# Both projections with 512-column matmuls, low parts of plain weight blocks by ScalarE and an accumulating DMA, bias rows copied DRAM to DRAM

## The chip, the cores and the metric

The kernel runs on one core of a Trainium2 chip. The metric is the device time of one execution in microseconds (us), the median of several runs. Engines: TensorE (PE in the profile), VectorE (DVE), ScalarE (ACT), GpSimd (POOL, used here almost only to issue DMAs) and SyncE (SP, which issues the loads of weights). Each engine works through its own instructions in order and waits on semaphores for the others.

## What is computed

One decoder layer on 512 tokens of width 2048, all in float32: an input projection (2048 to 12288), a gated convolution and three dilated attentions with a relative-position bias, an output projection (2048 to 2048), a LayerNorm, an up projection (2048 to 11264), a gated convolution with SiLU, a down projection (5632 to 2048) and a second LayerNorm.

```
proj = x @ w_in                                   # 512 x 2048 @ 2048 x 12288
u, gate_b, gate_c, q, k, v = split(proj)
y_conv = gate_b * causal_conv3(gate_c * u, conv_mix_w)
y_attn = mix of three dilated window attentions (scores + bias(rel_bias))
x1 = layernorm(ALPHA * x + concat(y_conv, y_attn) @ w_out)
up = causal_conv3(x1 @ w_up, ffn_conv_w) + ffn_conv_b     # 2048 x 11264
a, g = split(up)
out = layernorm(ALPHA * x1 + (silu(g) * a) @ w_down)
```

The change touches the two widest products, `x @ w_in` and `x1 @ w_up` ("both projections"), and the table of bias rows.

## The kernel before

**Two-part numbers.** A float32 operand is cut into a high part, rounded to fp32r by ScalarE, and a low part, the rest. A product is three matmuls: high by high, high weight by low activation, low weight by high activation.

**Both projections** take the output features in pairs of two 128-feature blocks: 48 pairs for `w_in` (phase 1), 44 for `w_up` (phase 3; each pair is a value block and its gate block). Tokens are cut into two halves of 256, the 2048 inputs into two halves of 1024, so that a pair is a 2 x 2 by 2 x 2 block product. It is computed with seven products instead of eight (Winograd's form of Strassen's method). `PROD` lists them: product 1 is A11 by B11, 5 is S1 by T1, 6 is S2 by T2, 3 is S4 by B22, 7 is S3 by T3, 4 is A22 by T4, 2 is A12 by B21. The activations' S are sums of token blocks, computed once per phase; the weights' T are differences of weight blocks, computed anew for every pair by VectorE. The order is `MAIN` = 1, 5, 6, 3, 7, 4, 2, below called steps 0 to 6. Steps 0, 3 and 6 use a plain weight block (kind "B"), the other four a T.

**One product** (`product`, lines 317 to 329) is 8 chunks of three matmuls of 256 columns, weights stationary: `op.hi` by the activation's high part (326), `op.hi` by its low part (327), `op.lo` by its high part (328). All three add into one half of a PSUM bank; a pair uses two banks, "m" for the sums x2 and x1, "n" for x4 and x3. ScalarE copies some of the running sums out in between (`snap`, 374), and VectorE adds copy and bank to the output tile o (`bands`, 572 and 581).

**Weight preparation** (`Op`, lines 162 to 196). `front` computes T where there is one (VectorE, 181) and the high part (ScalarE, 191); `back` computes the low part (VectorE, 194). High and low tiles lie in a ring of `RING` = 4, so the front of a weight block is issued when PE has finished the product four steps earlier, and its back when the next front has been issued. Raw weights are loaded by SP into `RAWS` = 3 tiles of 1 MB; a tile is loaded anew when every part made of it is done.

**After a pair** `later(n, ...)` and `tick` put work some products later into the program. In phase 3 `done3` issues, one step after the next pair's step 0, two scaled copies by ScalarE (1006); the convolution's taps by VectorE (589), SiLU by ScalarE (1010), the gate's product by VectorE (1013) and a store to `act_d` by POOL (1014) follow in the next three steps. In phase 1 `done1` stores q, k, v to `qkv_d` by POOL (611) or runs the mixer's convolution.

**A few pairs are different.** At the start of each phase five pairs have products 1 and 2 taken ahead (`run_pre`) and one pair is computed with the plain eight products (`run_plain`), while S and T operands aren't there yet. That leaves 42 of 48 pairs in phase 1 and 38 of 44 in phase 3 with all seven products in `run_pairs`.

**Bias rows** (`bias_setup`, 548): in phase 1, after the last mixer pair, three small tables of 8 heads by up to 383 values are computed in an o tile on 8 partitions, and POOL writes each to `seq_d` in DRAM with every row repeated 128 times (563). The attention reads them later with a skewed access pattern.

The output and down projections (`tm_unit`, lines 421 to 423) use 512-column matmuls with the activations stationary; their weights have kind "W".

Of the kernel before, what the change touches and what calls it, by code (L numbers as in the profile page):

```python
# [12 lines left out]
F32 = mybir.dt.float32  # L13
# [5 lines left out]
P = 128  # L19
D = 2048  # L20
S = 512
# [32 lines left out]
UNIT = 1024  # L54
NWARM = 6
XS, XL, XF, XR = 4, (0, 0, 1, 4), (1, 2, 3, 6), (7, 9, 11, 12)
HF, HR = 3, (6, 8, 10, 12)
# [17 lines left out]
def _plain(seq):  # L75
    return isinstance(seq[0], str)
# [5 lines left out]


class Chunks:
    def __init__(self, tiles, j):
        self.tiles, self.j = tiles, j

    def __getitem__(self, at):
        k = at[1]
        if isinstance(k, slice):  # L90
            return self.tiles[k.start // 2][:, self.j]
        return self.tiles[k // 2][:, self.j, k % 2]


@with_exitstack
def layer_kernel(ctx: ExitStack, tc: tile.TileContext, xT, x, w_in, w_out, w_up, w_down, cw, fw, lnp, lnc, table,
# [32 lines left out]
    act_d = dram.tile([P, FT, S], F32, name="act_d")  # L129
    seq_d = dram.tile([3, NH, P, 384], F32, name="seq_d")  # L130
    stA_d = dram.tile([NH, S, 2], F32, name="stA_d")
    stB_d = dram.tile([NH, S, 2], F32, name="stB_d")
# [29 lines left out]
    class Op:  # L162
        def __init__(self, kind, parts, box=None, ext=0):
            self.kind, self.parts, self.box, self.ext = kind, parts, box, ext
            for r, _ in parts:
                r.left += 1
            ops.append(self)
# [8 lines left out]
        def front(self):  # L176
            v = [self.view(i) for i in range(len(self.parts))]
            if self.kind[0] == "T":
                self.src = tt_tile()
                prev = v[1] if len(v) > 1 else self.box["T1" if self.kind == "T2" else "T2"]  # L180
                nc.vector.tensor_sub(self.src, v[0], prev)  # L181
# [9 lines left out]
            nc.scalar.activation(self.hi, self.src, AF.Copy)  # L191

        def back(self):
            nc.vector.tensor_sub(self.lo, self.src, self.hi.bitcast(F32))  # L194
            for r, _ in self.parts:
                r.left -= 1
# [110 lines left out]
    pairb = {}  # L307

    def region(p, name):
        rg = pairb.setdefault(p, {})  # L310
# [6 lines left out]
    def product(p, q, X, last):  # L317
        op = take()
        for q in q if isinstance(q, str) else [q]:
            xn, _, reg = PROD[q]  # L320
            xh, xl = X[xn]
            first = not _banks(q) & set(pairb.get(p, {}))
# [42 lines left out]

    def run_pairs(pl, X, stile, otile, bands, done, hook=None):
        for p, seq, pre in pl:
            if pre or _plain(seq):
                continue
            sn = {b: stile(b).rearrange("p (a t) -> p a t", a=2) for b in "mn"}  # L370
# [69 lines left out]
    def s_alloc(X, pools):  # L440
        for n in ("S2", "S4"):
            tiles = [None] * 4
            X[n] = (Chunks(tiles, 0), Chunks(tiles, 1))
        X["pools"] = pools
# [29 lines left out]
    def xtile(pool, n):  # L474
        return tuple(pool.tile([P, 8, 256], F32R, tag=n + s, name=nm(n + s)) for s in "hl")

# [54 lines left out]
    hook = schedule(todo)  # L531

    def keep1():
        return tp.tile([P, 2, 256], F32, tag="kp", name=nm("kp"), bufs=PRE1[0])

# [4 lines left out]
    nc.sync.dma_start(gb_t, lnc)  # L540

    def stile1(b):
        return tp.tile([P, 512], F32, tag="s" + b, name=nm("s" + b), bufs=2)

# [3 lines left out]
    def bias_setup(g=0):  # L548
# [9 lines left out]
        def finish():  # L558
# [16 lines left out]
    def bands1(p, o, b, ps, sn):  # L575
# [3 lines left out]
        for i in range(2):  # L579
            f, h = (i, i) if b == "m" else (i, 1 - i)  # L580
            nc.vector.tensor_add(ov[:, f, :, 64 * h:64 * h + 64],
                                 ps[:, 256 * i:256 * i + 256].rearrange("p (m r) -> p r m", r=4),
                                 sn[:, i].rearrange("p (m r) -> p r m", r=4))

    held = {}
# [26 lines left out]

    run_plain(plan1, X, otile1, done1, hook)
    run_pairs(plan1, X, stile1, otile1, bands1, done1)
    ph1.close()

# [217 lines left out]
    a1p = mkpool(a1s, "a1p")  # L834
    A1h = a1p.tile([P, 2, 8, 256], F32R, tag="h", name="A1h")
    A1l = a1p.tile([P, 2, 8, 256], F32R, tag="l", name="A1l")
    chp = mkpool(chs, "chp")
# [125 lines left out]
    X["S3"] = xtile(s3p, "S3")  # L963
    X["A11"], X["A12"] = (A1h[:, 0], A1l[:, 0]), (A1h[:, 1], A1l[:, 1])

# [23 lines left out]
    def act_first(p, q):  # L989
        if p < FT - 1:  # L990
            return
        if q == 2:
            act_load(0, xrp, "S1h", nc.gpsimd)
            act_load(1, xrp, "S1l", nc.gpsimd)
            for s in "hl":
                act[s] = a1p.tile([P, 2, 4, S], F32R, tag=s, name=nm("A" + s))
        if q in (6, 3):
# [22 lines left out]
    run_plain(plan3, X, otile3, done3, hook)  # L1020
    run_pairs(plan3, X, stile3, otile3, bands, done3, act_first)
    xrs.close()
# [177 lines left out]
```

## Time and profile before

| what | time |
|---|---|
| median of 3 runs | 2673.99 us (2672.46 to 2676.10) |
| the profiled execution, whole | 2674.91 us |
| its span | 2673.0 us, mean granted TensorE clock 0.992 |
| phase 1 (`w_in`) | from the start to about 1020 us |
| attention and output projection | about 1020 to 1290 us |
| phase 3 (`w_up`) | about 1260 to 2110 us |
| down projection, second LayerNorm | about 2110 to 2673 us |

The page lists the busy time of each engine, then the span in 40 slices, the DMA queues, the chain of waits that ended last, groups of instructions by line, and DMA issues. In a row of a group, "out<-in" are tile names, then come partitions x elements, the count, busy us and mean ns. Consecutive instructions of one engine overlap a little, so the mean of one is slightly more than the step from one to the next. A row of the stretches lists, for a window of the span, the busy us and the number of instructions of each engine, the granted clock, the DMA engines' share and GB/s.

### The profile page before, as it was taken

What the parts mean: (1) busy time and instruction counts of PE and PEld (TensorE: products, weight loads), DVE (VectorE), ACT (ScalarE), POOL (GpSimd) and SP (SyncE); (2) the same over time, 40 slices, a digit from 0 to 9 for tenths busy, and PEclk for the clock granted to TensorE, in tenths of its full rate; (3) what the DMA queues carried; (4) which work ended last, traced back from release to release, by engine and by line L of the source; (5) the groups of instructions that cost most, each with busy time, mean ns of one, the idle gap of its engine ahead of it and who ended that gap; (6) DMA issues with size and microseconds to landing.
All of it is one profiled execution on the core that took longest, in us unless ns stands there. A gap on an engine that the chain in (4) does not pass through costs nothing.

```text
span 2673.0 us, 45078 instructions
## 1 busy us (share of the span) xinstructions
PE 2624.3 (98%) x19114; PEld 2497.2 (93%) x19114; DVE 2015.5 (75%) x2293; ACT 1159.3 (43%) x1617; POOL 124.4 (5%) x214
## 2 busy tenths in 40 slices
PE   9999889999999999999999999999999999999998
PEld 8999789999999998888999999999999998888886
DVE  7987557777777777666899888888888875675557
ACT  5444334444444444434655555555555553222220
POOL 0000000000000002221000000000000000000000
PEclk9999989999999999999999999999999999999999
DMA  7433653333333338644543333333333354434331
GB/s 240 166 103 128 111 138 125 134 129 132 135 123 139 134 119 312 221 160 160 182 144 131 117 123 111 123 123 108 126 119 111 127 181 156 149 142 148 120 126 63
DMA packets 70905, 376.69 MB, mean 141 GB/s; under 512 B 10608, under 2 KB 14440, under 8 KB 36016
## 3 DMA queue, kind: packets, MB, share of 16 engines
q1 hardware_dynamic: 51680, 311.47, 34.0%
q0 software_dynamic: 19024, 62.34, 7.3%
q8 instruction: 150, 2.46, 0.4%
q14 instruction: 51, 0.42, 0.1%
HBM read 324.95 MB, written 48.81 MB: 140 GB/s over the span
## 4 chain that ended last, share of the span: by engine, by line
PE 88%; DVE 5%; DMA 4%; ACT 1%; issue 1%; SPq 0%; DVEq 0%; POOL 0%; ACTq 0%
PE bk L326 21%; PE bk L328 21%; PE bk L327 21%; PE bk L423 8%; PE bk L421 8%; PE bk L422 8%; DMA raw<-in_w_in_dram 2%; DMA seq_d<-o 2%; DVE wlo L194 1%; DVE tt L181 1%; PE bk L744 1%; PE bk L690 1%; PE bk L674 0%; ACT whi L191 0%; PE bk L736 0%
## 5 line engine op out<-in xcount | busy, mean ns | idle before, releaser
L191 ACT ACTIVATE whi<-raw 128x1024 fp32r<-128x1024 f32 x394 | 416.0, 1058 | 631.9 <-PE bk L423 219.0
L194 DVE TENSOR_TENSOR wlo<-raw,whi 128x1024 fp32r<-128x1024 f32 x394 | 480.7, 1223 | 216.0 <-ACT whi L191 215.9
L194 DVE TENSOR_TENSOR wlo<-tt,whi 128x1024 fp32r<-128x1024 f32 x360 | 440.5, 1224 | 210.1 <-ACT whi L191 209.5
L191 ACT ACTIVATE whi<-tt 128x1024 fp32r<-128x1024 f32 x360 | 379.6, 1054 | 220.1 <-PE bk L327 122.7
L326 PE MATMUL bk<-S,whi 128*128 128x256 f32 x1440 | 409.2, 284 | 12.4 <-ACT sm L374 11.5
L327 PE MATMUL bk<-S,whi 128*128 128x256 f32 x1440 | 408.4, 284 | 0.0
L328 PE MATMUL bk<-S,wlo 128*128 128x256 f32 x1440 | 408.4, 284 | 0.0
L326 PEld LDWEIGHTS bk<-S,whi 128*128 128x128 f32 x1440 | 277.5, 193 | 13.6 <-ACT sm L374 11.9
L327 PEld LDWEIGHTS bk<-S,whi 128*128 128x128 f32 x1440 | 277.5, 193 | 0.0
L328 PEld LDWEIGHTS bk<-S,wlo 128*128 128x128 f32 x1440 | 277.4, 193 | 0.0
L181 DVE TENSOR_TENSOR tt<-raw,tt 128x1024 f32<-128x1024 f32 x180 | 219.1, 1217 | 36.6 <-DMA raw<-in_w_in_dram 36.6
L326 PE MATMUL bk<-A22h,whi 128*128 128x256 f32 x752 | 212.8, 283 | 0.0
L327 PE MATMUL bk<-A22l,whi 128*128 128x256 f32 x752 | 212.8, 283 | 0.0
L328 PE MATMUL bk<-S3h,wlo 128*128 128x256 f32 x752 | 212.8, 283 | 0.0
L327 PE MATMUL bk<-S3l,whi 128*128 128x256 f32 x752 | 212.8, 283 | 0.0
L326 PE MATMUL bk<-S3h,whi 128*128 128x256 f32 x752 | 212.8, 283 | 0.0
L328 PE MATMUL bk<-A22h,wlo 128*128 128x256 f32 x752 | 212.8, 283 | 0.0
L328 PE MATMUL bk<-S1h,wlo 128*128 128x256 f32 x720 | 205.1, 285 | 6.2 <-DVE wlo L194 6.2
L326 PE MATMUL bk<-A1h,whi 128*128 128x256 f32 x720 | 205.2, 285 | 0.6 <-ACT S L932 0.6
L326 PE MATMUL bk<-S1h,whi 128*128 128x256 f32 x720 | 204.7, 284 | 0.0
L327 PE MATMUL bk<-S1l,whi 128*128 128x256 f32 x720 | 204.7, 284 | 0.0
L328 PE MATMUL bk<-A1h,wlo 128*128 128x256 f32 x720 | 204.4, 284 | 0.0
(225 smaller groups left out, 6435.4 us busy)
## 6 DMA issues: line engine op xcount, KB each, us to landing
raw<-in_w_in_dram SPq DMA_DIRECT2D x97, 1024.0 KB, 4.9
raw<-in_w_up_dram SPq DMA_DIRECT2D x89, 1024.0 KB, 5.3
raw<-in_w_down_dram SPq DMA_DIRECT2D x44, 1024.0 KB, 4.9
qkv_d<-o POOLq DMA_DIRECT2D x36, 512.0 KB, 4.3
raw<-in_w_out_dram SPq DMA_DIRECT2D x16, 1024.0 KB, 6.8
act_d<-z POOLq DMA_DIRECT2D x44, 256.0 KB, 5.2
qk<-qkv_d SPq DMA_DIRECT2D x7, 1536.0 KB, 10.3
ar<-act_d SPq DMA_DIRECT2D x9, 1024.0 KB, 7.0
```

Of the source, the lines that this page charges most:

```text
L181: nc.vector.tensor_sub(self.src, v[0], prev)
L191: nc.scalar.activation(self.hi, self.src, AF.Copy)
L194: nc.vector.tensor_sub(self.lo, self.src, self.hi.bitcast(F32))
L326: mm(ps, op.hi[:, w], xh[:, k], start=first and k == 0, stop=False, skip_group_check=True)
L327: mm(ps, op.hi[:, w], xl[:, k], start=False, stop=False, skip_group_check=True)
L328: mm(ps, op.lo[:, w], xh[:, k], start=False, stop=last and k == 7, skip_group_check=True)
L421: mm(banks[n], yh[:, tt], op.hi[:, w], start=first and i == 0, stop=False)
L422: mm(banks[n], yh[:, tt], op.lo[:, w], start=False, stop=False)
L423: mm(banks[n], yl[:, tt], op.hi[:, w], start=False, stop=last and i == 1)
L690: mm(ps[:, o:o + P], qk[:, 2 + 2 * g, rs], qk[:, 3 + 2 * g, rs], start=True, stop=True)
L744: nc.tensor.transpose(ps[:, i * P:(i + 1) * P], src[:, n, s:s + P], ident)
```

## The change

It has four parts.

1. **Wide products.** For pairs that have all seven products, `run_wide` and `product_wide` replace `run_pairs`' loop and `product`. High and low part of an activation now lie in one tile (`Wide`, `WideChunks`; method `both`), and one matmul of 512 columns multiplies `op.hi` with both. It writes a whole bank: the left half holds high by high, the right half high by low. The third matmul, `op.lo` by the high part, still has 256 columns and adds into the right half. A product is 8 x (512 + 256) columns in 16 matmuls instead of 24 of 256. A pair uses four banks, x1 to x4.
2. **Combining.** ScalarE copies whole banks (512 columns) after steps 0, 1 and 2, and x1 once more into a tile "u" in step 6. Each of the four 256-token blocks of a pair is then an addition of 512 columns (bank plus copy) and an addition of the two halves into o, both on VectorE. The block (f, h) = (0, 1), which uses u, is combined in step 6 and (0, 0) in the next pair's step 0. Tiles of the copies have their own tags in phase 1 and share the z tiles in phase 3.
3. **Low parts of plain blocks.** For weight blocks of kind "B", from the ninth on (`NLOW` = 8), `front` lets ScalarE write the negated rounded value into the low tile, and `back` issues, from POOL, a DMA of 512 KB from SBUF to SBUF that adds the raw weights to it. T blocks and the kind "W" keep VectorE's subtraction.
4. **Bias rows.** The small table goes to `seq1_d` first (8 rows), and a second DMA, DRAM to DRAM, writes the 128 copies to `seq_d` with the copies' index outermost.

Three places of the order of instructions, before and after. The first is ScalarE in phase 3, from the last instruction of step 6 of one pair on (before), and from the weight block issued in step 6 on (after). whi and wlo are high and low tiles, bk a PSUM bank, z a copy of a bank or a scaled copy of o. Before:

```order
L191 ACTIVATE whi_17823<-raw_17670 128x1024
L374 ACTIVATE z_17829<-bk_2193_17831 128x256
L191 ACTIVATE whi_17859<-tt_17857 128x1024
L1006 ACTIVATE z_17864<-o_17827,fw_t 128x512
L1006 ACTIVATE z_17865<-o_17827,fw_t 128x512
L374 ACTIVATE z_17829<-bk_2199_17868 128x256
L191 ACTIVATE whi_17896<-tt_17894 128x1024
L1010 ACTIVATE z_17865<-z_17865 128x512
L374 ACTIVATE z_17830<-bk_2193_17831 128x256
L191 ACTIVATE whi_17930<-raw_17670 128x1024
```

After, the same stretch:

```order
L220 ACTIVATE whi_14689<-raw_14567 128x1024
L222 ACTIVATE wlo_14690<-raw_14567 128x1024
L432 ACTIVATE z_14694<-bk_2248_14511 128x512
L454 ACTIVATE z_14715<-bk_2279_14698 128x512
L220 ACTIVATE whi_14719<-tt_14717 128x1024
L1120 ACTIVATE z_14725<-o_14644,fw_t 128x512
L1120 ACTIVATE z_14726<-o_14644,fw_t 128x512
L454 ACTIVATE z_14746<-bk_2286_14729 128x512
L220 ACTIVATE whi_14750<-tt_14748 128x1024
L1124 ACTIVATE z_14726<-z_14726 128x512
L454 ACTIVATE z_14775<-bk_2279_14698 128x512
L220 ACTIVATE whi_14777<-raw_14567 128x1024
```

New are the negated copy (L222) and, behind it, the copy u of x1 (L432); the copies of banks are twice as wide.

The second place is VectorE in phase 3 around the same point: tt are the T blocks. Before, from the first `bands` of a pair to the taps of its two blocks:

```order
L572 TENSOR_TENSOR o_19207<-bk_2334_19018,z_18980 128x512
L181 TENSOR_TENSOR tt_19237<-raw_18884,raw_19050 128x1024
L194 TENSOR_TENSOR wlo_19204<-raw_19050,whi_19203 128x1024
L572 TENSOR_TENSOR o_19207<-bk_2328_18981,z_18979 128x2x256
L181 TENSOR_TENSOR tt_19274<-raw_19050,tt_19173 128x1024
L194 TENSOR_TENSOR wlo_19240<-tt_19237,whi_19239 128x1024
L589 SCALAR_TENSOR_TENSOR z_19245<-o_19207,fw_t,z_19245 128x511
L589 SCALAR_TENSOR_TENSOR z_19245<-o_19207,fw_t,z_19245 128x510
L194 TENSOR_TENSOR wlo_19277<-tt_19274,whi_19276 128x1024
```

After, from the second block of a pair to the taps of its gate (z_15629 is u):

```order
L435 TENSOR_TENSOR z_15494<-bk_2403_15446,z_15494 128x512
L1137 TENSOR_TENSOR o_15579<-z_15494 128x256
L228 TENSOR_TENSOR wlo_15602<-tt_15599,whi_15601 128x1024
L435 TENSOR_TENSOR z_15629<-bk_2426_15582,z_15629 128x512
L1137 TENSOR_TENSOR o_15579<-z_15629 128x256
L210 TENSOR_TENSOR tt_15652<-raw_15366,raw_15502 128x1024
L435 TENSOR_TENSOR z_15463<-bk_2430_15607,z_15463 128x512
L1137 TENSOR_TENSOR o_15579<-z_15463 128x256
L210 TENSOR_TENSOR tt_15683<-raw_15502,tt_15599 128x1024
L228 TENSOR_TENSOR wlo_15655<-tt_15652,whi_15654 128x1024
L701 SCALAR_TENSOR_TENSOR z_15661<-o_15579,fw_t,z_15661 128x511
L701 SCALAR_TENSOR_TENSOR z_15661<-o_15579,fw_t,z_15661 128x510
```

The low part of a plain block is gone from VectorE; the addition that reads u stands ahead of T3 (L210, tt_15652) and of the last block's additions.

The third place is POOL at the bias rows. Before:

```order
L606 DMA yc_d<-o_2942 128x1024
L551 DMA tb<-in_table_dram 32x24
L563 DMA seq_d<-o_2983 1024x1x383
L611 DMA qkv_d<-o_3172 128x2x512
L563 DMA seq_d<-o_3208 1024x1x255
```

After:

```order
L226 DMA wlo_2776<-raw_2568 128x1024
L226 DMA wlo_2797<-raw_2618 128x1024
L664 DMA seq_d<-o_2727 8x383
L665 DMA seq_d<-seq_d 128x8x383
L226 DMA wlo_2876<-raw_2755 128x1024
L723 DMA qkv_d<-o_2825 128x2x512
L226 DMA wlo_2961<-raw_2755 128x1024
```

The first L664 row writes `seq1_d`. The accumulating DMAs (L226) share POOL's queue with both copies of the bias rows and with the stores.

The core of the diff:

```diff
+NLOW = 8
+    def product_wide(p, q, X, last):
+        op = take()
+        xn, _, reg = PROD[q]
+        first = reg not in pairb.get(p, {})
+        ps = wide_region(p, reg)
+        for k in range(8):
+            w = slice(k * P, (k + 1) * P)
+            mm(ps.rearrange("p (a t) -> p a t", a=2), op.hi[:, w], X[xn].both(k), start=first and k == 0, stop=False,
+               skip_group_check=True)
+            mm(ps[:, 256:], op.lo[:, w], X[xn][0][:, k], start=False, stop=last and k == 7, skip_group_check=True)
+        return op
...
+    WSUM = {(0, 0): ("x2", 1), (1, 1): ("x1", 5), (0, 1): ("x4", "x1"), (1, 0): ("x3", 6)}
+    def run_wide(p, seq, X, stile, otile, put_block, done, hook):
+        WNEED = {(0, 0): {1, 2}, (1, 1): {5, 6, 7}, (0, 1): {4, 6, 7}, (1, 0): {3, 6}}
+        def combine(block):
...
+            reg, other = WSUM[block]
+            if other == "x1":
+                u = stile("u")
+                nc.scalar.activation(u, pairb[p][other], AF.Copy)
+            else:
+                u = sn[other]
+            nc.vector.tensor_add(u, pairb[p][reg], u)
+            put_block(p, box["o"], block, u)
...
+            op = product_wide(p, q, X, PROD[q][2] not in {PROD[j][2] for j in left})
+            if q in (1, 5, 6):
+                sn[q] = stile(str(q))
+                nc.scalar.activation(sn[q], pairb[p][PROD[q][2]], AF.Copy)
+            for block, need in WNEED.items():
+                if block not in sent and not need & left:
+                    sent.add(block)
+                    later(2, functools.partial(combine, block))
+            free(op)
+            tick()
...
+            self.by_dma = kind[0] == "B" and len(ops) >= NLOW
...
             nc.scalar.activation(self.hi, self.src, AF.Copy)
+            if self.by_dma:
+                nc.scalar.activation(self.lo, self.src, AF.Copy, scale=-1.0)
 
         def back(self):
-            nc.vector.tensor_sub(self.lo, self.src, self.hi.bitcast(F32))
+            if self.by_dma:
+                nc.gpsimd.dma_start(self.lo, self.src, accum_op=OP.add)
+            else:
+                nc.vector.tensor_sub(self.lo, self.src, self.hi.bitcast(F32))
...
-            nc.gpsimd.dma_start(seq_d[g, :, :, :b - a], mk[:, None].to_broadcast([NH, P, b - a]))
+            nc.gpsimd.dma_start(seq1_d[g, :, :b - a], mk)
+            nc.gpsimd.dma_start(seq_d[g, :, :, :b - a].rearrange("h p n -> p h n"),
+                                seq1_d[g, None, :, :b - a].to_broadcast([P, NH, b - a]))
...
+    def block3(p, o, block, u):
+        f, h = block
+        nc.vector.tensor_add(o[:, 2 * f + h], u[:, :256], u[:, 256:])
```

`block1`, its counterpart in phase 1, writes with a stride of four tokens for the dilated groups. The remaining lines put the two parts of each activation operand into one tile.

More of the change, by code (lines that the diff above doesn't have):

```diff
@@ L80, in _banks, with __init__, __getitem__, both @@
     return {"m" if PROD[i][2] in ("x1", "x2") else "n" for i in (q if isinstance(q, str) else [q])}
+class Wide:
+    def __init__(self, t):
+        self.t = t
+    def __getitem__(self, j):
+        return self.t[:, j]
+    def both(self, k):
+        return self.t[:, :, k]
 class Chunks:
@@ L92, in __getitem__, with __init__, both @@
         return self.tiles[k // 2][:, self.j, k % 2]
+class WideChunks:
+    def __init__(self, tiles):
+        self.tiles = tiles
+    def __getitem__(self, j):
+        return Chunks(self.tiles, j)
+    def both(self, k):
+        return self.tiles[k // 2][:, :, k % 2]
 @with_exitstack
@@ L474, in xtile @@
     def xtile(pool, n):
-        return tuple(pool.tile([P, 8, 256], F32R, tag=n + s, name=nm(n + s)) for s in "hl")
+        return Wide(pool.tile([P, 2, 8, 256], F32R, tag=n, name=nm(n)))
     ph1 = ExitStack()
@@ L992, in act_first @@
         if q == 2:
[L993 to L996, printed above, removed]
+            t = xrp.tile([P, 2, 4, S], F32, tag="S1", name=nm("ar"))
+            for i in range(2):
+                act[i] = t[:, i]
+                nc.gpsimd.dma_start(act[i], act_d[:, 4 * i:4 * i + 4, :])
+            t = a1p.tile([P, 2, 2, 4, S], F32R, tag="A1", name=nm("A"))
+            act["h"], act["l"] = t[:, 0], t[:, 1]
         if q in (6, 3):
@@ L1020, in layer_kernel @@
     run_plain(plan3, X, otile3, done3, hook)
-    run_pairs(plan3, X, stile3, otile3, bands, done3, act_first)
+    def block3(p, o, block, u):
+        f, h = block
+        nc.vector.tensor_add(o[:, 2 * f + h], u[:, :256], u[:, 256:])
+    run_pairs(plan3, X, stile3, otile3, bands, done3, act_first, block3)
     xrs.close()
```

54 lines of the change are left out of this document (44 added, 10 removed).

## The prediction

> **What bounds the kernel now.** First the page's engines and its chain of waits.
>
> ```profile
> PE 2624.3 (98%) x19114; PEld 2497.2 (93%) x19114; DVE 2015.5 (75%) x2293; ACT 1159.3 (43%) x1617; POOL 124.4 (5%) x214
> PE 88%; DVE 5%; DMA 4%; ACT 1%; issue 1%; SPq 0%; DVEq 0%; POOL 0%; ACTq 0%
> ```
>
> PE is busy nearly always, and the chain of waits runs through PE for 88%. But a busy PE is no measure of its pace, so next come stretches of the span: us, then busy us (and count) of PE, PEld, DVE, ACT, POOL, the granted clock, the DMA share, GB/s.
>
> ```profile
> 0.00:70.00 70.00, 63.56 (x470) 60.68 (x471) 54.86 (x68) 39.44 (x54) 0.70 (x6) 0.98 0.68 231
> 270.00:400.00 130.00, 106.30 (x808) 103.30 (x808) 71.45 (x71) 39.77 (x52) 6.96 (x8) 0.89 0.58 125
> 400.00:700.00 300.00, 300.00 (x2502) 300.00 (x2502) 220.29 (x214) 126.28 (x163) 10.00 (x14) 1.00 0.37 130
> 1400.00:2080.00 680.00, 679.75 (x5664) 679.54 (x5664) 597.45 (x614) 356.75 (x474) 18.92 (x35) 1.00 0.36 120
> 2200.00:2600.00 400.00, 400.00 (x1766) 331.22 (x1765) 234.06 (x275) 104.09 (x107) 6.45 (x12) 1.00 0.39 142
> ```
>
> In phase 1, 2502 matmuls of 256 columns in 300 us are one per 119.9 ns; phase 3 has 5664 in 680 us, 120.1 ns. The down projection's 512-column matmuls come every 226.5 ns. Twice the columns cost 106.6 ns more, so 13.3 ns of each matmul don't depend on its columns. PE sets the pace in both phases; VectorE is at 73% and 88%, ScalarE at 42% and 52%. From 270 to 400 us PE does 808 matmuls where 130 us hold 1084: 276 x 0.1199 = 33 us are lost there, the only large hole. Those losing it, from the list of waits (waiter, released by: total us, times, longest):
>
> ```profile
> DVE tt L181 <- DMA raw<-in_w_in_dram: 36.6, 3, 15.5
> DVE o L572 <- DMA seq_d<-o: 11.7, 1, 11.7
> PE bk L326 <- ACT sm L374: 11.5, 2, 10.6
> ```
>
> While the bias rows are written, raw weights come late and o stays occupied.
>
> **Wide matmuls.** A product's chunk was three matmuls, 359.7 ns; now it is 226.5 + 119.9 = 346.4. A step takes 8 x 346.4 ns = 2.77 us for 2.88, a pair of seven steps 19.40 for 20.14: 0.745 less. If nothing else intervenes that is 42 x 0.745 = 31 us in phase 1 and 28 us in phase 3. The moving operand is now two pieces of 256 columns, which no row shows; I take the contiguous operand's price, the nearest row. At worst the whole 13.3 ns is lost again.
>
> The Trainium skill ("TensorE: Matmul & The Clock Gate", section "Back-to-back issue gap") gives a warm gap of columns / 2.4 + 2.5 ns, so only 2.5 ns per matmul saved: 11 us over both phases instead of 60. The trace disagrees (119.9 where that gives 109.2, 226.5 where it gives 215.8), and the measurement decides.
>
> **VectorE and ScalarE.** Rows of the groups by line: tile shapes, count, busy us, mean ns.
>
> ```profile
> L191 ACT ACTIVATE whi<-raw 128x1024 fp32r<-128x1024 f32 x394 | 416.0, 1058 | 631.9 <-PE bk L423 219.0 <-PE bk L327 190.9 <-DVE zz L887 131.8
> L194 DVE TENSOR_TENSOR wlo<-raw,whi 128x1024 fp32r<-128x1024 f32 x394 | 480.7, 1223 | 216.0 <-ACT whi L191 215.9
> L181 DVE TENSOR_TENSOR tt<-raw,tt 128x1024 f32<-128x1024 f32 x180 | 219.1, 1217 | 36.6 <-DMA raw<-in_w_in_dram 36.6
> L572 DVE TENSOR_TENSOR o<-bk,z 128x512 f32<-128x512 f32 x86 | 58.8, 684 | 0.0
> L589 DVE SCALAR_TENSOR_TENSOR z<-o,fw_t,z 128x511 f32<-128x511 f32 (+1 forms) x176 | 131.8, 749 | 10.5 <-ACT z L1006 7.4
> L737 ACT ACTIVATE vt<-bk 128x512 f32<-128x512 f32 x24 | 12.4, 588 | 0.0
> L1006 ACT ACTIVATE z<-o,fw_t 128x512 f32<-128x512 f32 x88 | 66.5, 805 | 3.6 <-DVE o L572 3.1 <-DVE o L350 0.5
> L1010 ACT ACTIVATE z<-z 128x512 f32<-128x512 f32 x44 | 27.8, 632 | 11.7 <-DVE z L589 11.7
> ```
>
> Per pair VectorE loses 3 low parts (3.67 us) and two `bands` (1.37), and gains four bank additions (2.74) and four additions of halves. 512 columns take 0.684 and 1024 take 1.22, so 256 should take 0.42: 1.68. It is 0.6 us lighter. ScalarE gains 3 x 1.06 and, for four copies of 0.38, four of 0.59: 4 us per pair. Neither becomes the bound by its sum (in phase 3 some 17.1 and 14.6 of 19.4 us). Their order matters more.
>
> **The accumulating DMA.** No row shows one. The nearest, with KB and median us from issue to landing, and the software queue's packets, MB and share of 16 engines' span:
>
> ```profile
> qkv_d<-o POOLq DMA_DIRECT2D x36, 512.0 KB, 4.3
> yc_d<-o POOLq DMA_DIRECT2D x4, 512.0 KB, 3.3
> raw<-in_w_up_dram SPq DMA_DIRECT2D x89, 1024.0 KB, 5.3
> q0 software_dynamic: 19024, 62.34, 7.3%
> ```
>
> A copy of the same size takes 3.3 to 4.3 us. The accumulating one reads two operands. The queue's share is 0.073 x 16 x 2673 = 3122 us of an engine for 62.34 MB, so 32 KB on each of 16 engines take 1.64 us; one more pass makes 4.9 to 5.9. The ends are 3.3 (the second read costs nothing) and 8.6 (twice the slower copy). I take L = 5.0, from the quicker copy, since by the order below no load of raw weights runs beside the DMA that matters.
>
> The Trainium skill ("Collectives: The Full Stack", section "The bandwidth ceiling: the fold count and why AG ≠ RS ≠ AR") holds that a reducing transfer is half as fast as a copy because it reads two sources, not because of the addition. No run here shows it yet; it would give the same 4.9 to 5.9, not the 3.3.
>
> **Where it must be ready.** Call the end of step 6 zero and a step 2.77. Rows of ScalarE in phase 3 (start, duration) show how much room a pair had:
>
> ```profile
> 1499.10 1.05 ACT L191 ACTIVATE whi<-tt 128x1024 fp32r<-128x1024 f32 x1
> 1500.05 1.51 ACT L1006 ACTIVATE z<-o,fw_t 128x512 f32<-128x512 f32 x2
> 1501.70 0.38 ACT L374 ACTIVATE z<-bk 128x256 f32<-128x256 f32 x1
> 1503.22 0.63 ACT L1010 ACTIVATE z<-z 128x512 f32<-128x512 f32 x1 [0.19 <-DVE z L589]
> 1504.58 0.38 ACT L374 ACTIVATE z<-bk 128x256 f32<-128x256 f32 x1 [0.72 <-PE bk L328]
> ```
>
> Instructions in a row start about 0.1 us before the last has ended, the scaled copies never waited, and 0.72 us were idle before the copy of step 2.
>
> A plain block's weights are needed three steps after its front, its low part 0.23 (the first wide matmul) later: at 8.54. High part and negated copy take 2.1, so the issue is at 2.2 and L may be 6.3. That holds for the blocks issued after steps 3 and 6. The one issued after step 2, B21 for the next step 6, is worse, because of the new order. ScalarE does high part, negated copy and only then u (2.0 to 2.6). VectorE, in order, waits for u: addition to 3.3, halves to 3.75, T3 to 4.9, the last block to 5.9. In phase 3 ScalarE's scaled copies wait for that block: 6.0 to 7.5, where they could start at 4.5 (step 0's end, bank copy, high part of a T). Behind them are step 1's bank copy (8.0) and a high part (9.0); VectorE's low part and two taps end at 9.7, SiLU at 10.4, step 2's bank copy at 10.9, then B21's high part (11.9), negated copy (12.8), and POOL's issue at 12.9. PE needs it at 6 x 2.77 + 0.23 = 16.85: L may be 3.95. T3 ends at 4.9, so the raw tile that it frees is loaded by 10.2 (5.3 us, above); the other tile is freed by this DMA itself. In phase 1 there is no scaled copy or SiLU, the issue comes at 11.2 and L may be 5.65.
>
> So phase 3's pair lasts 12.9 + L + 2.54 (the rest of step 6) as soon as that is over 19.40: with L = 5.0, 20.44 us, 0.28 more than before (168 x 120.1 ns = 20.17): 38 x 0.28 = 11 us lost where 28 were to be gained. Phase 1 keeps its 31.
>
> **Bias rows.** Before:
>
> ```profile
> seq_d<-o POOLq DMA_DIRECT2D x1, 1532.0 KB, 40.5
> seq_d<-o POOLq DMA_DIRECT2D x2, 1020.0 KB, 29.1
> tb<-in_table_dram POOLq DMA_DIRECT2D x1, 3.0 KB, 2.8
> ```
>
> The writes read 8 partitions. With the copies' index outermost and a source in DRAM I expect the raw loads' rate (1 MB in 5.3 us): 5 to 8 us each, and o free after a small DMA of about 2.8. But POOL waits for that one, and the next accumulating DMA is behind the copies: about 2.4 us late for the first, 1 to 3 for the others. I leave 8 of the 33 us; ends 4 (raw loads' rate) and 33 (as slow as before).
>
> **The two beginnings.** In the first 70 us VectorE is busy for 54.9 (first row of stretches), and eight low parts leave it; but the DMA engines are at 0.68, and one-block raw tiles are freed only when their DMA has landed: load 5.3, copies 2.1, L 5.0 are 12.4 us for three tiles, 4.1 per step of 2.88, for about four steps. Phase 3 begins in the same way. I put 6 us for both, ends -5 and +20.
>
> **The sum.** -31 + 11 - 25 + 6 = -39 on the profiled execution's 2674.9 us: 2636, and 2635 for the median, which lies 0.9 lower. I forecast 2634.
>
> **Rivals.**
> - **The DMA is slow and becomes the bound** (L over 5.9). Each us of L costs 38 us in phase 3, and from 5.65 on about 42 x 1.25 more in phase 1. The sum crosses zero at L = 5.9 to 6.0. At 6.3 phase 3 loses 60, phase 1's gain is spent, and with 15 from the bias rows and 6 for the beginnings the time is 2725; at 8.6, where all three plain blocks stall, it is about 3000. For it: `qkv_d<-o`'s 4.3 plus a pass is 5.9, and addition may be slower than copying. Against: the DMA engines are at 0.36. Chance 0.28.
> - **The DMA is as quick as a copy** (L up to 4.3). Phase 3 gains 16 to 29, the time is 2580 to 2605. For: 3.3 for yc_d; against: two reads. Chance 0.16.
> - **The wide matmul saves nothing or little** (two-piece operand). Phase 1 gains 0, phase 3's chain stays: 11 - 25 + 6 = -8, 2666. Against it stand the two paces above. Chance 0.07. The skill's 2.5 ns would end there too: phase 1 would gain 6 us instead of 31, 2660.
>
> **How the numbers follow.** Forecast, L between 4.3 and 5.6, bias rows and beginnings within their ends: 2605 to 2662, chance 0.42. Odd cases between: 0.07. The range of 8 in 10 runs from 2590 (L = 4.0) to 2725 (L = 6.3); below lie about 0.06, above 0.14. Within 0.2% (5 us, about what a measurement of this kernel can tell from no change): 0.07, from the slow DMA's near end and the useless wide matmul. Faster: 0.42 + 0.16 + 0.06 = 0.64. Slower: 0.29.
>
> **What would show it.** Right: stretches of phase 1 with one 512- and one 256-column matmul per 346 ns and a pair in 19.4 us; in phase 3 a pair in about 20.4 us with PE waiting once per pair, in step 6, for the low tile, and VectorE waiting for u; accumulating DMAs of about 5 us; no 10 us hole near 300 us. Wrong: a landing far from 5.0, PE waits in phase 1's pairs, or phase 3 at 19.4.

## The result, and the profile after

The changed kernel takes 2766.9 us (median of 4 runs, 2756.7 to 2769.8) where the kernel before takes 2674.9: the ratio is 1.034, with a 95% interval of 1.031 to 1.037. The forecast was 2634 us with a range of 2590 to 2725: wrong in sign, and outside the range.

First the page of the changed kernel: engines, the accumulating DMA's row (KB, median us from issue to landing), its queue (packets, MB, share), and the chain of waits.

```profile
PE 2624.5 (95%) x14634; PEld 2278.1 (82%) x14634; DVE 1928.8 (70%) x2451; ACT 1482.5 (54%) x1891; POOL 364.1 (13%) x491
wlo<-raw POOLq DMA_DIRECT2D x274, 512.0 KB, 5.0
q0 software_dynamic: 57824, 206.03, 35.6%
PE 62%; DMA 17%; issue 14%; DVE 2%; POOL 2%; ACT 2%; POOLq 0%; SPq 0%; DVEq 0%; ACTq 0%
```

The chain ran through TensorE for 88% before; now it does for 62%, and DMA has 17% of it. The median landing is the 5.0 us of the prediction. Where the time went is seen in the stretches that the prediction showed of the kernel before (same columns).

```profile
0.00:70.00 70.00, 56.13 (x377) 52.84 (x378) 38.97 (x54) 42.60 (x57) 7.76 (x14) 0.90 0.90 255
270.00:400.00 130.00, 114.40 (x615) 96.47 (x614) 79.28 (x95) 66.26 (x76) 22.53 (x28) 0.93 0.77 204
400.00:700.00 300.00, 299.31 (x1706) 260.55 (x1705) 216.71 (x244) 187.19 (x214) 50.87 (x61) 1.00 0.79 211
1400.00:2080.00 680.00, 641.54 (x3740) 559.79 (x3738) 545.04 (x667) 445.62 (x545) 98.09 (x126) 0.99 0.72 185
2200.00:2600.00 400.00, 394.85 (x1823) 328.91 (x1822) 256.73 (x308) 136.95 (x153) 19.27 (x31) 1.00 0.48 163
```

In the first 70 us TensorE does 377 matmuls instead of 470, at a granted clock of 0.90 instead of 0.98, with the DMA engines at 0.90. The steady part of phase 1 (third row) is full. From 1400 to 2080 us (fourth row) TensorE is idle for 39 us, where it hardly was before; 12 of them still belong to the beginning of phase 3.

Products of the two projections are the same and in the same order in both kernels, so the start of each, counted from its phase's first, can be compared. The table gives the difference to before in us (minus is earlier) at five marks: the first wide pair and the end of each phase, and between them product 127 of phase 1, behind the bias rows. It also has all runs of the study.

| run | median us | ratio to before, 95% | ph. 1: first wide pair | behind bias rows | end | ph. 3: first wide pair | end |
|---|---|---|---|---|---|---|---|
| after | 2766.9 | 1.031 to 1.037 | +37.7 | +24.9 | +19.0 | +40.8 | +67.0 |
| e1_vector_lows | 2637.7 | 0.985 to 0.988 | +1.6 | -34.0 | -45.2 | -0.1 | +1.3 |
| e2_dma_in_wide_pairs | 2684.3 | 1.003 to 1.006 | -0.2 | -12.3 | -21.0 | -0.3 | +27.1 |
| e3_bias_alone | 2643.6 | 0.987 to 0.990 | +0.1 | -31.6 | -31.6 | -0.6 | -0.6 |
| e4_dma_lows_alone | 2833.7 | 1.059 to 1.062 | +36.4 | +80.2 | +87.6 | +46.7 | +69.3 |
| e5_phase3_two_blocks | 2742.9 | 1.023 to 1.029 | +0.9 | -34.1 | -45.3 | -0.3 | +102.1 |
| e6_u_early | 2657.9 | 0.992 to 0.995 | +1.6 | -14.4 | -22.0 | -1.0 | +3.5 |
| e8_one_piece | 2636.7 | 0.984 to 0.987 | +1.5 | -33.7 | -44.9 | -0.2 | +0.5 |
| e9_bias_on_sync | 2675.1 | 1.000 to 1.002 | +2.5 | -21.4 | -28.4 | -1.0 | +27.2 |
| e10_store_later | 2672.3 | 0.999 to 1.001 | +0.4 | -34.7 | -45.9 | -0.2 | +34.9 |
| e13_u_early_store_later | 2645.5 | 0.987 to 0.990 | +1.0 | -11.4 | -16.8 | -1.1 | -7.7 |
| e11_phase3_one_block | **2621.3** | 0.979 to 0.982 | -0.1 | -35.7 | -46.9 | 0.0 | -14.2 |
| e14_dma_in_half_done_pairs | 2681.3 | 1.002 to 1.004 | +22.7 | -12.4 | -23.6 | +24.0 | +25.1 |

So of the 90 us that the profiled execution is longer (2765.3 for 2674.9), 78 are lost before the first wide pair of either phase, in products whose matmuls the change left alone. In these two stretches TensorE is idle 52 us longer than before, 47.5 us of it in 14 waits for a low tile that a DMA writes. The other 27 us are a slower pace: about the same number of matmuls (1032 and 1066) keeps it busy 13.6 and 13.0 us longer, at a mean granted clock of 0.89 and 0.90 instead of 0.99. What TensorE waits for there, from the list of waits between 60 and 140 us (total us, times, longest), and two DMA rows from the issue of one of these low parts at 100.0 us:

```profile
PE bk L381 <- DMA wlo<-raw: 11.5, 3, 4.8
...
raw<-in_w_in_dram SPq DMA_DIRECT2D x1, 1024.0 KB, 6.6
wlo<-raw POOLq DMA_DIRECT2D x1, 512.0 KB, 9.5
```

The accumulating DMA is issued 0.1 us after a 1 MB load of raw weights and lands in 9.5 us, not 5.0. Its product comes 6 us after the issue, so TensorE waits for it.

### The profile page after: what moved, and what is told of

Read it like the earlier page. It is cut to its first block, busy times and chain, and to the rows that moved or that the text cites. A ratio compares the mean times of both kernels' runs of the same rounds, so it can differ in the third digit from the quotient of the medians.

```text
span 2763.4 us, 37379 instructions
## 1 busy us (share of the span) xinstructions
PE 2624.5 (95%) x14634; PEld 2278.1 (82%) x14634; DVE 1928.8 (70%) x2451; ACT 1482.5 (54%) x1891; POOL 364.1 (13%) x491
## 4 chain that ended last, share of the span: by engine, by line
PE 62%; DMA 17%; issue 14%; DVE 2%; POOL 2%; ACT 2%; POOLq 0%; SPq 0%; DVEq 0%; ACTq 0%
PE bk L357 22%; DMA wlo<-raw 15%; PE bk L359 12%; PE bk L524 7%; PE bk L522 7%; PE bk L523 7%; PE bk L381 1%; POOL wlo L226 1%; PE bk L379 1%; PE bk L380 1%; DMA raw<-in_w_in_dram 1%; POOL act_d L1128 1%; ACT whi L220 1%; ACT wlo L222 1%; PE bk L856 1%
## 5 line engine op out<-in xcount | busy, mean ns | idle before, releaser
L357 PE MATMUL bk<-S,whi 128*128 128x512 f32 x2560 | 908.8, 398 | 1.0 <-ACT s L454 1.0
L359 PE MATMUL bk<-S,wlo 128*128 128x256 f32 x2560 | 721.7, 282 | 21.1 <-DMA wlo<-raw 21.1
L357 PE MATMUL bk<-A,whi 128*128 128x512 f32 x1920 | 680.0, 396 | 0.0
L359 PE MATMUL bk<-A,wlo 128*128 128x256 f32 x1920 | 543.4, 283 | 36.2 <-DMA wlo<-raw 35.8
L359 PEld LDWEIGHTS bk<-S,wlo 128*128 128x128 f32 x2560 | 486.8, 190 | 22.8 <-DMA wlo<-raw 22.8
L357 PEld LDWEIGHTS bk<-A,whi 128*128 128x128 f32 x1920 | 360.3, 188 | 85.0 <-issue 1.5
L226 POOL DMA_DIRECT2D wlo<-raw x274 | 235.9, 861 | 1458.3 <-ACT wlo L222 1285.7
L359 PEld LDWEIGHTS bk<-A,wlo 128*128 128x128 f32 x1920 | 362.4, 189 | 51.9 <-DMA wlo<-raw 51.6
L222 ACT ACTIVATE wlo<-raw 128x1024 fp32r<-128x1024 f32 x274 | 286.3, 1045 | 0.0
L228 DVE TENSOR_TENSOR wlo<-raw,whi 128x1024 fp32r<-128x1024 f32 x120 | 146.4, 1223 | 132.2 <-ACT whi L220 132.0
L210 DVE TENSOR_TENSOR tt<-raw,tt 128x1024 f32<-128x1024 f32 x180 | 219.3, 1218 | 4.4 <-DMA raw<-in_w_in_dram 4.4
L522 PE MATMUL bk<-whi,A 128*128 128x512 f32 x480 | 186.7, 389 | 0.0
L524 PE MATMUL bk<-whi,A 128*128 128x512 f32 x480 | 186.7, 389 | 0.0
L381 PE MATMUL bk<-S,wlo 128*128 128x256 f32 x352 | 107.8, 306 | 31.0 <-DMA wlo<-raw 31.0
```

The lines of the kernel that those rows point to most:

```text
L222: nc.scalar.activation(self.lo, self.src, AF.Copy, scale=-1.0)
L226: nc.gpsimd.dma_start(self.lo, self.src, accum_op=OP.add)
L357: mm(ps.rearrange("p (a t) -> p a t", a=2), op.hi[:, w], X[xn].both(k), start=first and k == 0, stop=False, skip_group_check=True)
L359: mm(ps[:, 256:], op.lo[:, w], X[xn][0][:, k], start=False, stop=last and k == 7, skip_group_check=True)
L381: mm(ps, op.lo[:, w], xh[:, k], start=False, stop=last and k == 7, skip_group_check=True)
L522: mm(banks[n], yh[:, tt], op.hi[:, w], start=first and i == 0, stop=False)
```

## The experiments

### First: which part of the change loses the time

e1 takes the accumulating DMA away and keeps all the rest:

```diff
-NLOW = 8
+NLOW = 10 ** 9
```

> Wide matmuls and the new bias rows kept, all low parts by VectorE again (no accumulating DMA). Theory A (the accumulating DMA at the beginnings of both projections and behind the bias rows loses the time): the first product of phase 1's wide pairs starts where it did before (within 8 us, where after was 38 later), phase 1 gains about 40 in all; in phase 3 VectorE becomes the bound (17.1 us of work a pair plus 3 x 1.22 = 20.8), about 0.6 x 37 = 22 us lost; sum 2640 to 2665. Theory B (the wide pairs with their four-bank combination lose it themselves): still over 2735. Theory C (the loop in phase 3 with B21's DMA is most of it): 2700 to 2730.

Measured: 2637.7 us, 129 less than after and 2 less than the lowest that was expected. Both beginnings are back to those of before, phase 1 ends 45 us early. Theory B falls: wide pairs with their four-bank combination cost nothing that shows. Phase 3 lost only 1.3 us, not 22: VectorE is full, but TensorE hardly waits (us, then busy us and count of PE, PEld, DVE, ACT, POOL, clock, DMA share, GB/s):

```profile
400.00:700.00 300.00, 300.00 (x1701) 260.08 (x1700) 262.13 (x288) 144.46 (x167) 10.70 (x15) 1.00 0.38 132
1400.00:1900.00 500.00, 493.82 (x2771) 423.26 (x2770) 494.84 (x594) 278.09 (x347) 13.52 (x25) 1.00 0.35 118
```

e2 keeps the accumulating DMA in the wide pairs alone:

```diff
-            self.by_dma = kind[0] == "B" and len(ops) >= NLOW
+            self.by_dma = low == "dma"
...
-            Op(k, parts[k], box)
+            Op(k, parts[k], box, 0, "dma" if 1 in seq and k[0] == "B" else "")
```

> The change, with low parts by accumulating DMA only in the pairs that run wide; the blocks of the early products, the plain pair and the five half-done pairs have VectorE's low parts again, in both phases. Theory A: both beginnings return to those of before (within 5 us each), 70 to 78 us less than after: 2688 to 2697. Theory B or C: the beginnings weren't the loss, at most 20 us less than after: 2745 or more.

Measured: 2684.3, 83 us less than after; both beginnings as before. Theory A holds. What is left against e1 is 24 us in phase 1 (behind the bias rows, and 8 in its last pair) and 26 in phase 3's pairs.

e3 is before with the bias rows' two DMAs (the diff's lines on `seq1_d` and in `bias_setup`), nothing else.

> The kernel before with the new way of the bias rows alone (small DMA, then copies from DRAM to DRAM), no wide pairs, no accumulating DMA. Theory A (the rows themselves are quick; what is left of the hole in after comes from the accumulating DMAs behind them in the same queue): 25 to 33 us less than before, 2642 to 2650. Rival (the DRAM to DRAM writes still hold up the raw weights): 8 to 15 less, as in after: 2660 to 2667.

Measured: 2643.6, 30 us less, as theory A says. The 130 us with the hole are now full, with 1072 matmuls where before had 808:

```profile
270.00:400.00 130.00, 130.00 (x1072) 128.10 (x1071) 95.08 (x92) 53.40 (x69) 8.66 (x12) 1.00 0.47 159
```

e4 is before with the accumulating DMA (the parts of the diff in `Op`), nothing else.

> The kernel before with the low parts of plain blocks by ScalarE and accumulating DMA alone (256-column matmuls, old combination, old bias rows). Theory A: both beginnings lose their 70 to 78 us, and the DMAs queued behind the bias rows' 40.5 and 29.1 us writes add 20 to 50: 2765 to 2805. Theory B (the wide pairs are the loss): within 15 of before, 2675 to 2690. Phase 3's steady pairs: no u stands in ScalarE's row here, so the loop over B21 should be gone and the pair stay at 20.17.

Measured: 2833.7, 29 us more than expected at most. The beginnings lose 36 and 47 us, as in after. The bias stretch loses 44 more on top of the 33 that before loses, where three DMAs behind the old writes of the bias rows land in 33, 31 and 23 us. Steady pairs of phase 3 lose 0.6 us each, where I expected none: u isn't the whole story of their wait.

### Second: phase 3's pair, the bias rows, the matmul's operand

e5 gives two of the three plain blocks of phase 3's wide pairs to the DMA, and all else to VectorE:

```diff
-            Op(k, parts[k], box)
+            Op(k, parts[k], box, 0, "dma" if src is w_up and 1 in seq and q in (1, 3) else "")
```

> e1_vector_lows, with the low parts of B11 and B22 of phase 3's wide pairs by accumulating DMA (B21, needed in step 6, and all of phase 1 by VectorE). Theory A (e1's phase 3 was bound by VectorE, busy for 445 of 450 us; B11's and B22's DMAs have room for 6.3 us and aren't in the loop over step 6): the pair falls from 20.15 to between 19.4 and 19.8, 14 to 28 us less than e1: 2610 to 2624. Rival (any accumulating DMA in phase 3 makes TensorE wait): 2637 or more, with waits of TensorE for the low tile.

Measured: 2742.9, 105 us more than e1: a clear miss, and the most telling run. A pair takes 22.8 us, and all of the loss is in step 0 (5.91 us instead of 2.80), whose block is B11. Rows of POOL and then of TensorE, each its own view (start, duration, what it did, idle before and releaser):

```profile
1616.16 0.58 POOL L1128 DMA_DIRECT2D act_d<-z  x1 [14.85 <-DVE z L1127]
1616.73 0.87 POOL L226 DMA_DIRECT2D wlo<-raw  x1
```

```profile
1622.09 0.40 PE L357 MATMUL bk<-A,whi 128*128 128x512 f32 x1
1624.46 0.38 PE L359 MATMUL bk<-A,wlo 128*128 128x256 f32 x1 [1.97 <-DMA wlo<-raw]
1624.69 0.40 PE L357 MATMUL bk<-A,whi 128*128 128x512 f32 x1
...
1625.04 0.39 PE L357 MATMUL bk<-A,whi 128*128 128x512 f32 x1
...
1625.38 0.56 PE L357 MATMUL bk<-A,whi 128*128 128x512 f32 x1
...
1625.95 0.63 PE L357 MATMUL bk<-A,whi 128*128 128x512 f32 x1
1626.38 0.41 PE L359 MATMUL bk<-A,wlo 128*128 128x256 f32 x1
1626.59 0.63 PE L357 MATMUL bk<-A,whi 128*128 128x512 f32 x1
```

The store of the pair before stands ahead of B11's DMA in POOL's program and waits for VectorE; B11's DMA follows it by 0.57 us and lands at 1624.4, 7.7 us later, while product 0 is due at 1622.1. The second cost is below: 0.9 us after a wait of 2.0 the chunk's pitch goes from 0.35 to 0.64 us, so the clock falls for about three microseconds. The stretch from 1624.4 to 1628.4 us, with the columns of the stretches above, has a mean granted clock of 0.63:

```profile
1624.40:1628.40 4.00, 3.94 (x15) 3.36 (x16) 3.58 (x6) 0.32 (x1) 0.85 (x1) 0.63 0.74 132
```

In the wide pairs of phase 3 the trace has 22 such stretches of 3.4 us at a granted clock of 0.5, which at half pace cost about 39 us, and 38 waits of 78.8 us together.

e6 is e2 with u copied a step earlier:

```diff
+        def copy_u():
+            sn["u"] = stile("u")
+            nc.scalar.activation(sn["u"], pairb[p]["x1"], AF.Copy)
...
+                    if WSUM[block][1] == "x1":
+                        later(1, copy_u)
```

> e2_dma_in_wide_pairs, with the copy u of the shared bank one step earlier in ScalarE's row (ahead of step 6's high part and negated copy). The loop as the prediction has it (u late, so VectorE's additions late, so ScalarE's scaled copies late, so B21's issue late): phase 3's pair falls from 20.8 to between 19.4 and 19.9, 33 to 53 us less than e2: 2631 to 2651. Rival (the landing of 5 us, or the traffic, is the bound whatever the order): within 8 of e2, 2676 to 2692. Phase 1 as in e2 by both.

Measured: 2657.9, 26 us less than e2, 7 short of what was expected: a pair falls from 20.9 to 20.2. So u's late copy is a part of the loop, but step 0 still takes 3.42 us: B11's DMA lands in 6.5, with the store 1.1 us ahead of it and B21's DMA 2.2.

e8 is e1 with a chunk's high and low tokens side by side:

```diff
-        return Wide(pool.tile([P, 2, 8, 256], F32R, tag=n, name=nm(n)))
+        return Wide(pool.tile([P, 8, 2, 256], F32R, tag=n, name=nm(n)))
```

> e1_vector_lows, with high and low tokens of a chunk side by side, so that a 512-column matmul reads one contiguous piece of 512 instead of two of 256, 2048 columns apart. If the two pieces cost the 3.5 to 9.5 ns by which the 512-column matmul is over the down projection's 226.5 ns: its pitch falls from 236 to about 227, 8 x 9 ns x 7 x 42 = 21 us less in phase 1, phase 3 stays with VectorE: 2613 to 2625. If not: 2633 to 2641, pitch 230 to 236 as before.

Measured: 2636.7, the same as e1. The two pieces of the operand cost nothing.

e9 is e2 with the bias rows' second DMA issued by SyncE (`nc.gpsimd.dma_start(seq_d` becomes `nc.sync.dma_start(seq_d`).

> e2_dma_in_wide_pairs, with the bias rows' second DMA (DRAM to DRAM) issued by SyncE, so that no accumulating DMA stands behind it in POOL's queue and POOL doesn't wait for the small DMA. If the queue is the cause of what is left of the hole (from product 71 to 127 e2 loses 22 us more than e1): 12 to 22 less than e2, 2662 to 2672. If the traffic of the copies itself delays the accumulating DMA: within 6 of e2, 2678 to 2690.

Measured: 2675.1, 9 us less than e2, between the two expectations: about 9 of the 22 us come back by product 127. POOL's queue is a part of it; the rest stays open (the writes' traffic, or the raw loads that now stand behind them on SyncE).

### Third: what stands beside B11's DMA, and a kernel without it

e10 is e5 with the store issued a step later:

```diff
-            nc.gpsimd.dma_start(act_d[:, j, :], cv[0])
+            later(1, lambda: nc.gpsimd.dma_start(act_d[:, j, :], cv[0]))
```

> e5_phase3_two_blocks with one thing moved: the store of act_d is issued a step later, behind B11's accumulating DMA in POOL's queue instead of 0.6 us ahead of it. Theory Q (B11's DMA lands in 7.7 us because it stands behind the store's 256 KB in the same queue, and TensorE waits for it in step 0): it lands in about 5, before step 0 begins; the pair falls from 22.8 to 19.4 to 19.8: 2610 to 2630. Rival (the accumulating DMAs are late from traffic or from their place in ScalarE's row): 2720 or more.

Measured: 2672.3, 71 us less than e5, and 42 more than expected at most. Neither theory is right alone: B11's DMA, now first in the queue, still takes 7.5 us, so the store ahead of it was not all that made it slow. What the order gave is an issue 0.7 us earlier, measured from step 0. That shortens the 38 waits from 78.8 to 45.0 us, and stretches at half clock fall from 22 to one: TensorE is idle 34 us less and busy 34 us less for the same matmuls, so half of the gain is pace. The DMA rows between 1620.5 and 1622.2 us show what runs beside it: a 1 MB load issued 0.9 us ahead, the store 0.5 us behind.

```profile
raw<-in_w_up_dram SPq DMA_DIRECT2D x1, 1024.0 KB, 5.9
wlo<-raw POOLq DMA_DIRECT2D x1, 512.0 KB, 7.5
act_d<-z POOLq DMA_DIRECT2D x1, 256.0 KB, 7.6
```

e13 is e6 with the same edit.

> e6_u_early with the store of act_d a step later. Theory Q: B11's DMA, which still costs 0.6 us a pair in step 0 (3.42 us instead of 2.80), has one transfer less ahead of it; the pair falls from 20.2 to 19.5 to 19.8, 15 to 25 us less than e6: 2633 to 2643. Rival (B21's accumulating DMA 2 us ahead is what holds B11's): within 6 of e6, 2652 to 2664.

Measured: 2645.5, 12 us less than e6, a little short in the total; phase 3 gains 11. In its pairs B11's DMA lands in 5.7 us, behind B21's alone, the wait in step 0 is gone (2.85 us), and a pair takes 19.86 us, TensorE's own pace. Theory Q holds here.

e11 is e5 with `q == 3` in place of `q in (1, 3)`: only B22, which is issued alone.

> e5_phase3_two_blocks with only B22's low part of phase 3's wide pairs by accumulating DMA (B11 back on VectorE). B22's DMA has no other within 7 us ahead of it in the queue and landed in 4.8 to 5.2. Theory: VectorE's sum falls from 20.2 (e1) to about 19.2, so TensorE is the bound or near: pair 19.6 to 19.8, 15 to 22 us less than e1: 2615 to 2625. Rival (any accumulating DMA here makes TensorE wait): 2637 or more.

Measured: 2621.3, 16 us less than e1 and 53 less than before: it beats both kernels. Its windows and its DMA row:

```profile
270.00:400.00 130.00, 130.00 (x731) 110.89 (x731) 113.79 (x127) 61.15 (x71) 8.68 (x12) 1.00 0.50 159
400.00:700.00 300.00, 300.00 (x1701) 260.18 (x1700) 263.58 (x289) 144.08 (x168) 10.74 (x15) 1.00 0.38 132
1400.00:1900.00 500.00, 500.00 (x2831) 433.53 (x2831) 479.56 (x583) 309.11 (x382) 35.53 (x50) 1.00 0.50 148
...
wlo<-raw POOLq DMA_DIRECT2D x38, 512.0 KB, 4.8
```

TensorE is full in both projections; a pair takes 19.79 us in either. With one low part taken off it, VectorE has 4% of slack, and the DMA lands in 4.8.

e14 is e1 with the accumulating DMA only for B22 of the ten half-done pairs (`1 not in seq` in e2's condition).

> e1_vector_lows with accumulating DMAs only for the one plain block (B22) of each of the ten half-done pairs (five in each phase) that run with 256 columns ahead of the wide ones. Theory A1 (each such DMA is late by itself, as a 1 MB load of raw weights starts beside it and its raw tile is held until it lands): after's 26 us in phase 1 and 20 in phase 3 come back, 2675 to 2690. Theory A2 (they were late from what the early products and the plain pair had piled up): at most 10 us more than e1, 2636 to 2648.

Measured: 2681.3, 44 us more than e1, as theory A1 says: ten DMAs cost 44 us. The DMA rows at one issue (87.0 us), then TensorE's wait for it:

```profile
raw<-in_w_in_dram SPq DMA_DIRECT2D x1, 1024.0 KB, 6.5
wlo<-raw POOLq DMA_DIRECT2D x1, 512.0 KB, 8.9
```

```profile
95.94 0.39 PE L381 MATMUL bk<-S,wlo 128*128 128x256 f32 x1 [2.73 <-DMA wlo<-raw]
```

The load was issued 0.14 us before the DMA. So the late landing isn't a backlog from the early products: each DMA meets a load of its own. That the load is what slows it is argued from the rows side by side; no kernel was tried in which only the load was moved. All accumulating DMAs of the runs with no other DMA of POOL's in flight or issued beside them bear it out, by the time to the nearest issue of a load of raw weights: a median of 4.6 us to land with none within 3 us (101 DMAs), 4.8 with a load about 2.7 us behind the DMA (295), 5.3 with 1.4 us (117), 6.1 with 0.8 us (57), and 8.6 to 10.0 with one within 0.3 us of the issue (23).

## Why the prediction was wrong

**The step that failed is "The two beginnings": 6 us forecast, ends -5 and +20, 78 measured.** It counted three raw tiles by 5.3 + 2.1 + 5.0 us and spread the loss over four steps. It kept the landing at 5.0 beside DMA engines at 0.68 and looked only at the early one-block tiles. The runs show 8.7 to 10.0 us there, where a 1 MB load starts within 0.3 us of each DMA, and one such wait in each half-done pair (e14: 44 us for ten), besides those of the early products. It also reckoned with full pace throughout; 27 of the 78 us are matmuls at a lower clock. The sentence "no load of raw weights runs beside the DMA that matters" was read from the steady pair and wasn't asked of the beginnings.

**Bias rows: 25 of 33 us forecast, about 8 kept.** Their own cost was judged well: alone they bring 30 us (e3). The remainder of 8 was mis-sized, it is about 25: from the first wide pair to product 127 after gains 12.8 us, some 5 of them from the wide pairs. The wait list of the changed kernel around 320 us shows it, and POOL's rows show why.

```profile
PE bk L359 <- DMA wlo<-raw: 8.5, 1, 8.5
```

```profile
317.19 0.55 POOL L664 DMA_DIRECT2D seq_d<-o  x1 [3.73 <-DVE o L662]
322.50 0.95 POOL L665 DMA_DIRECT2D seq_d<-seq_d  x1 [4.76 <-DMA seq_d<-o]
323.44 0.95 POOL L226 DMA_DIRECT2D wlo<-raw  x1
```

The prediction saw that POOL waits for the small DMA, here 4.8 us, and that the next accumulating DMA stands behind the copies, but it put only 2.4 us on that. Behind the 1.5 MB of copies the DMA takes 13.1 us to land, some 8 more than alone, as the DMA rows of these two issues show:

```profile
seq_d<-seq_d POOLq DMA_DIRECT2D x1, 1532.0 KB, 10.9
wlo<-raw POOLq DMA_DIRECT2D x1, 512.0 KB, 13.1
```

**Wide matmuls: 0.745 us a pair forecast, 0.37 measured in e1, 0.75 in parts of after and e2.** The chunk of 347 ns (230 + 117 from start to start) that was forecast exists; in other stretches it is 353 (236 + 117). The whole gain is then 16 us in phase 1 and not 31. Which of the two holds changes mostly where TensorE waited, now and then without; e8 shows that the operand's two pieces aren't the cause. It stays open. The rival "saves little" isn't right either: e1 beats e3 by 6 us, though it pays about 6 between the phases, where the output projection now arrives ahead of its loaded operand. As for the 2.5 ns that the Trainium skill ("TensorE: Matmul & The Clock Gate", section "Back-to-back issue gap") allows an isolated matmul beyond its columns: the pair of 347 ns has 768 columns, 320 ns at 2.4 GHz, and so 13.5 ns for each of the two matmuls, 16.5 in the slower rhythm. The measurement decides.

**Phase 3's loop: right in kind, wrong in the block and too small.** Forecast +11 us, measured +26. Waits of VectorE for u and of TensorE for a low tile, from 1400 to 2080 us of the changed kernel:

```profile
DVE z L435 <- ACT z L432: 33.1, 28, 1.4
PE bk L359 <- DMA wlo<-raw: 26.3, 28, 1.4
```

Both come once per pair, as forecast. POOL's rows, and TensorE's of the same pair:

```profile
1633.89 0.85 POOL L226 DMA_DIRECT2D wlo<-raw  x1 [9.84 <-ACT wlo L222]
1634.43 0.88 POOL L1128 DMA_DIRECT2D act_d<-z  x1
1635.79 0.85 POOL L226 DMA_DIRECT2D wlo<-raw  x1 [0.47 <-ACT wlo L222]
```

```profile
1620.78 0.40 PE L357 MATMUL bk<-A,whi 128*128 128x512 f32 x1
1621.73 0.39 PE L359 MATMUL bk<-A,wlo 128*128 128x256 f32 x1 [0.56 <-DMA wlo<-raw]
...
1624.42 0.40 PE L357 MATMUL bk<-S,whi 128*128 128x512 f32 x1
```

B21's DMA is issued 13.1 us after step 0's start at 1620.78; 12.9 was forecast. But it lands in 4.6, in time. The one that is late is the next, B11's for step 0 (after A, the product with S follows): it is issued 1.9 us behind B21's, with the store of 256 KB between them, and lands in 7.1. The prediction gave each DMA the same L and never put two of them and the store into one queue. A pair so takes 20.9 us, for 20.44 forecast.

**What was right:** L itself (5.0 median), phase 1's steady pairs without waits, VectorE and ScalarE not becoming the bound by their sums, and bias copies far quicker than the old writes, though at 9.6 and 10.9 us they took longer than the 5 to 8 expected. **Not foreseen:** 8 us in phase 1's last pair, where a DMA lands late behind the loads of the attention. e1, without that wait, pays 6 of them behind the phase, so it's worth little.

**The rivals.** "The DMA is slow and becomes the bound" came nearest, but put the threshold on the median and the loss into the steady pairs. The median was as forecast, and most of the loss lay at places where few DMAs run, in landings of 9 to 10 us and the lower clock there.

**Do the parts add up?** By the products' starts in after, yes: +38 in the first beginning, -13 from there to behind the bias rows, -14 from there to phase 1's last pair, +8 in that pair, +1 between the phases, +41 in the second beginning, +26 in phase 3's pairs and +3 behind them are the 90 us.

## What to carry to other kernels

A DMA's landing has no single value: ask of each issue what stands ahead of it in its queue and which loads start within the same microsecond, above all at the start of a phase, where buffers are short. Work taken off an engine that has slack (VectorE at 73%) buys nothing, and put on a DMA it adds a latency to the path; where the engine was full (phase 3 of e1), one block moved, issued alone, was worth 16 us, and a second one cost 122, a third of it through the lower clock. Moving a part of a change at a time shows such an optimum; the whole change hides it.

## What the runs showed of the hardware

- **The accumulating DMA's landing (512 KB)** goes by what is issued beside it. With no other DMA of POOL's in flight it takes 4.6 us in the median where no load of raw weights starts within 3 us, 4.8 to 5.3 with a load 2.7 to 1.4 us behind it, 6.1 with one 0.8 us behind, and 8.6 to 10.0 with one within 0.3 us. It takes 5.7 us behind one of its kind 1.9 us ahead, 6.5 to 7.1 with a 256 KB store in the queue as well, and 13.1 behind 1.5 MB of copies.
- **In queue time it costs twice a copy.** From e1 to e11, which adds 38 of them, the software queue's share goes from 6.6% to 11.0%: 3.0 us on each of 16 engines per DMA, where e1's copies take 1.5 for as many bytes. That a reducing transfer is half as fast as a copy (the Trainium skill, "Collectives: The Full Stack", section "The bandwidth ceiling: the fold count and why AG ≠ RS ≠ AR", which says it of a ReduceScatter) agrees with this. From issue to landing it is less than twice: 4.6 us alone for 3.3 to 4.3 of a copy, a little under the 4.9 to 5.9 that the prediction worked out. The reason that the page gives, two sources, isn't shown here.
- **Short waits cost the clock.** In the wide pairs of phase 3 of e5, 29 of TensorE's waits left it idle for 1.7 to 2.5 us, and 19 of these were followed by a stretch of 3.4 us at a granted clock of 0.5, with matmuls at about half the pace (0.64 us a chunk for 0.35). Length alone doesn't decide it, since 10 of the 29 were not. None of 140 waits of 0.4 to 1.7 us in the same place of seven runs was followed by one. The Trainium skill ("TensorE: Matmul & The Clock Gate", section "HAM oscillation — how this bites in real kernels") warns of idle gaps above about 3.4 us; here 2 us were enough.
- **A matmul rhythm with two values**, 347 and 353 ns a chunk, that holds for dozens of products and changes mostly at a wait. Its cause wasn't found.
